# An encoder layer on two requests: projection traced at three times the pace, and two attentions that alternate on score banks of their own

## The chip, the core and the metric

The kernel runs on one NeuronCore of a Trainium2 chip. TensorE (PE; PEld is its weight load) multiplies matrices into PSUM, which has eight banks of 512 float32 values on each of 128 partitions. VectorE (DVE), ScalarE (ACT) and GpSimd (POOL) do the elementwise work, GpSimd only in SBUF. SyncE (SP) and ScalarE issue the DMAs. The engines run side by side, each through its own queue in order, and wait for each other by semaphores. The metric is the device time of one execution in microseconds; shown is the median of the runs.

## The reference

One transformer layer (DEPTH = 1, width 1024) is applied to two requests with the same weights: a prompt of 1024 positions and a sample of 512. Each gets 16 learned meta tokens in front, which are dropped at the end.

```python
n = rms_norm(x, g_mix);  proj = n @ w_in            # 18 column tiles of 128
# group A: 8 query heads of 64 on 2 key heads, per-head RMS norm of q and k, 2-D rotary
s = einsum('bqhgd,bkhd->bhgqk', qblk, ka) * scale;  oa = softmax(s) @ va
# group B: 4 heads, two softmax maps each, 1-D rotary
a = softmax(s0) - lam * softmax(s1);  ob = rms_norm(a @ vb, g_subln) * (1 - lam_init)
x = x + concat(oa, ob) @ w_out
n = rms_norm(x, g_ffn)
gate = conv3(n @ w_ff_gate) + conv_b                # width 3 over positions
x = x + (gelu(gate) * (n @ w_ff_up)) @ w_ff_down    # d_ff = 2816
return rms_norm(x, g_final)[:, N_META:]
```

## The kernel before

All is float32. A dense matmul takes each operand as a rounded part and a remainder (`split`, lines 120 to 124; hi on ScalarE, lo on VectorE or GpSimd) and sums three products (`mm3`, lines 127 to 131: hi·hi, hi·lo, lo·hi). Its lines 129, 130 and 131 stand for all dense work, and the tile name tells which: `ps_mm<-xhi,w_hi`, `ps_p`, `ps_mm<-a_hi,w_hi` (the last product of the feed-forward).

In the code s = 0 is the prompt and s = 1 the sample. The parts are generators, and each `yield` gives the columns that TensorE went through:

- `projection(s)`, lines 157 to 371: RMS statistics, then the 18 column tiles of `w_in`, with rotary and head norm on the other engines. q, k and v go to DRAM as hi and lo parts (SP, lines 258 and 345 to 353).
- `attention(s)`, lines 374 to 588. `softmax` (line 419) is given 128 queries (or 102 to 114 in group B): scores against all keys into one wide PSUM tile (lines 426 and 427; two banks for the sample, three for the prompt), the eviction with scale and row maximum on VectorE (line 430), the exponential on ScalarE (line 433). `weighted_v` (line 436) transposes the probabilities through `ps_t` (line 447), splits them (lines 123 and 124) and multiplies with v into one `ps_o` bank (lines 457 to 462, the tail at 471). Group A goes in blocks of 512 queries (lines 509 to 544): 8 for the sample, 16 for the prompt, and two short blocks each for one halo position. Group B (lines 546 to 588) adds two scalings on ScalarE (lines 553 and 556) and a sum on GpSimd (line 557) for each tile, and a norm of the output (lines 562 to 569), whose sum of squares takes the `ps_o` bank once more (line 566): 8 blocks for the sample, 12 for the prompt. q, k and v are loaded from DRAM on SP (lines 395, 414 and 416).
- `mixer_out(s)`, lines 609 to 668: the output projection and the residual, with h loaded from DRAM (line 640).
- `conv_glu(s)`, lines 671 to 798: the feed-forward in groups of two d_ff tiles, and the final norm.

`trunk_kernel` strings them together (lines 914 to 949). The sample's projection runs first. Then `merge` (line 801) traces the sample's attention beside the prompt's projection, 1 to 1.1 by columns, the projection 20,000 columns ahead; it ends with the attention, and the rest of the projection is drained. Then `merge` traces the prompt's attention beside the sample's `mixer_out` and `conv_glu`, 1 to 1, the attention 60,000 columns ahead; the rest of those is drained. The prompt's `mixer_out` and `conv_glu` come last and alone.

The traced order isn't the order of the instructions. It is a priority: a planner (`schedule_with_timeline_sim`) goes through a simulated time and gives each engine the first instruction in this order that is ready. `issue_after` forbids to issue before a given instruction on the same engine.

PSUM comes in pools that are opened and closed in the order of tracing. While both run, the sample's attention and the prompt's projection hold 2 banks for scores, 2 for `ps_t`, 1 for `ps_o` and 3 for `ps_mm`. After that, the prompt's attention has 3 for scores, 2 and 1, and the dense work beside it has 2. All these pools are closed and opened anew between the two stages, in one stack.

Of the kernel before, what the change touches and what calls it, by code (L numbers as in the profile page):

```python
# [12 lines left out]
F32 = mybir.dt.float32  # L13
# [4 lines left out]
PSUM = bass.MemoryType.PSUM  # L18
DRAM = bass.MemoryType.DRAM

P = 128
# [52 lines left out]
class Psum:  # L74


    def __init__(self, tc, name, **bufs):
        self.tc, self.name, self.count = tc, name, 0
        self.es, self.last = ExitStack(), ExitStack()
        self.pools = {tag: self.open(self.es, tag, b) for tag, b in bufs.items()}  # L80

    def open(self, es, tag, bufs):
        self.count += 1
        return es.enter_context(self.tc.tile_pool(name=f"{self.name}{self.count}_{tag}", bufs=bufs, space=PSUM,
                                                  reuse_waits="tile"))

    def relay(self, **bufs):
        self.last.close()
        for tag, b in bufs.items():
            self.pools[tag] = self.open(self.last, tag, b)  # L90

    def close(self):
        self.last.close()
        self.es.close()

    def tile(self, rows, cols, tag):
        return self.pools[tag].tile([P, 512], F32, name=f"ps_{tag}", tag=tag)[:rows, :cols]

    def wide(self, rows, chunks, cols):

        return self.pools["s"].tile([P, chunks, 512], F32, name="ps_s", tag="s")[:rows, :, :cols]


def pool(ctx, g, name, bufs, side):
# [269 lines left out]
def attention(ctx, g, s, side):  # L374
    nc, tc = g.nc, g.tc
# [3 lines left out]
    nch = -(-n // 512)  # L379
# [39 lines left out]
    def softmax(q, k, l):  # L419

        M = q[0].shape[-1]
        p = pp.tile([P, ne], F32, name="p", tag="p")[:M]
        ps = g.psum.wide(M, nch, kw)
        for i in range(nch):
            kc = k[:, i * kw:(i + 1) * kw]
            nc.tensor.matmul(ps[:, i], lhsT=q[0], rhs=kc, start=True, stop=False)  # L426
            nc.tensor.matmul(ps[:, i], lhsT=q[1], rhs=kc, start=False, stop=True)  # L427

        nm = sp.tile([P, 1], F32, name="nm", tag="nm")[:M]
        g.evicted = nc.vector.tensor_scalar(out=p.rearrange("p (i w) -> p i w", i=nch), in0=ps, scalar1=-HD ** -0.5,  # L430
                                            scalar2=3.0e38, op0=ALU.mult, op1=ALU.min, accum_out=nm).ins
        p = p[:, :n]
        nc.scalar.activation(p, p, AF.Exp, bias=nm, scale=-1.0, accum_out=l)  # L433
        return p

    def weighted_v(pl, v, diff):

        W = sum(p.shape[0] for p in pl)
        o = g.psum.tile(P, W, "o")
        v, v_tail = v  # L440

# [356 lines left out]
        yield 4 * cw  # L798


def merge(g, a, wa, b, wb, lead, hold):

    done = [0.0, lead]
    after, held = None, 0
    while True:
        i = 0 if b is None or done[0] / wa <= done[1] / wb else 1
        if i == (lead > 0) and held < hold:
            after, held = after or g.mark, held + 1
            order = g.tc.issue_after(after)
        else:  # L810
            order = nullcontext()
        try:
            with order:
                done[i] += next((a, b)[i])
        except StopIteration:
            if i == 0:
                break
            b = None


def drain(gen):
    for _ in gen:
        pass
# [3 lines left out]
PADD = 8  # L827
ML = 2
NRAW, NW = 2, 3
R1, R2 = (1.0, 1.1), (1.0, 1.0)  # L830
LEAD1, LEAD2, HOLD, STATS = -20000.0, 60000.0, 4, 26


@with_exitstack
def trunk_kernel(ctx, tc, g):
# [75 lines left out]
        st.tail = hp  # L911
        return st

    g.psum = Psum(tc, "psa", mm=3)
    g.psum.relay(p=3, t=2)
    with ExitStack() as es0:
        p0 = projection(es0, g, 0, "left", "mm", "mm")
        with ExitStack() as es:
            p1 = projection(es, g, 1, "right", "p", "t")
            for _ in range(STATS):  # L920
                next(p1)
            next(p0)
            drain(p1)
        g.psum.relay(s=1, t=2, o=1)
        with ExitStack() as es1:
            merge(g, attention(es1, g, 1, "right"), R1[0], p0, R1[1], LEAD1, HOLD)
        drain(p0)
    g.psum.close()
    g.psum = Psum(tc, "psb", mm=2)
    g.psum.relay(s=1, t=2, o=1)  # L930
    with ExitStack() as es1:
        st1 = state(es1, 1, "right", True)

        def sample():
            yield from mixer_out(g, 1, st1, "right", True, "mm")
            yield from conv_glu(es1, g, 1, st1, "right", 1)
        f1 = sample()
        with ExitStack() as es0:
            merge(g, attention(es0, g, 0, "left"), R2[0], f1, R2[1], LEAD2, HOLD)
        drain(f1)  # L940
        g.psum.relay(s=6)
        st0 = state(ctx, 0, "left", False)
        drain(mixer_out(g, 0, st0, "left", False, "s"))
    xp = pool(ctx, g, "fx0", 1, "right")
    st0.x = [xp.tile([P, KT, SEQS[0] + 2], F32R, name=nm) for nm in ("xhi", "xlo")]
    g.psum.close()
    g.psum = Psum(tc, "psc", mm=8)
    drain(conv_glu(ctx, g, 0, st0, "right", 2))
    g.psum.close()


def rope_tables():
# [60 lines left out]
```

## Time and profile before

| | |
|---|---|
| Median of 3 runs | 2235.35 us (2234.18 to 2236.82) |
| Profiled execution | 2229.83 us; its span, first to last instruction, 2228.0 us |
| Mean granted TensorE clock | 0.977 |
| Instructions | 32312, of them 12442 matmuls |
| HBM read, written | 172.11 MB, 48.55 MB |

The profiled execution is one of its own, and all times in the views are counted from its first instruction. "Busy" of TensorE is modelled from start and size of each matmul, and a matmul at a lower granted clock is busy for longer; so busy time times granted clock is what was done at full speed. In a windows view, a row gives for a stretch its width, the busy time of each engine with the number of instructions in brackets, the granted clock (1.00 is full), the share of DMA engines busy, and GB/s. In a timeline, a row gives start, length, engine, line, operation and count, and in brackets how long the engine had been idle and what released it.

### The profile page before, as it was taken

Reading aid. Unit: us, or ns where it says so; the run is one execution under the profiler, and the core shown is the slowest. Engines: PE = TensorE matmul, PEld = TensorE weight load, DVE = VectorE, ACT = ScalarE, POOL = GpSimd, SP = SyncE. Lnnn points to the kernel's source line nnn. Section 1 sums busy time; section 2 is a strip of 40 time slices with the busy share of each in tenths; the row PEclk is TensorE's granted clock in tenths of the full one; section 3 lists DMA queues with packets and bytes.
Section 4 is the critical chain, followed back from the end, with each engine's and each line's share of the span. In section 5 each row is a group of like instructions: output and inputs, shape, how many; then the busy total and the mean of one; then the engine's idle time right before and its main releaser. Section 6 shows DMA issues by size and latency. Waiting matters only on the chain.

```text
span 2228.0 us, 32312 instructions
## 1 busy us (share of the span) xinstructions
PE 2131.8 (96%) x12442; PEld 1912.6 (86%) x12442; DVE 1269.7 (57%) x2235; ACT 1039.7 (47%) x1830; POOL 668.5 (30%) x514
## 2 busy tenths in 40 slices
PE   7898999986999999999999998999999999999997
PEld 6897999975898888889989986998888888888887
DVE  6535554454767677777777775774443344433346
ACT  6434555565656445567777775552112221112224
POOL 5862446431123111144444433330111000111004
PEclk9999999996999999999999998999999999999999
DMA  6663454443332322223333215621111111111112
GB/s 216 195 206 116 143 169 162 134 162 116 124 99 73 101 79 81 85 72 117 111 101 99 77 61 180 197 94 47 43 37 54 48 48 48 48 38 57 48 39 76
DMA packets 109794, 222.77 MB, mean 100 GB/s; under 512 B 11976, under 2 KB 63048, under 8 KB 109128
## 3 DMA queue, kind: packets, MB, share of 16 engines
q1 hardware_dynamic: 80840, 115.83, 15.9%
q10 hardware_dynamic: 28800, 104.87, 14.9%
q8 instruction: 98, 1.61, 0.3%
q14 instruction: 56, 0.46, 0.1%
HBM read 172.11 MB, written 48.55 MB: 99 GB/s over the span
## 4 chain that ended last, share of the span: by engine, by line
PE 83%; DVE 6%; DMA 3%; ACT 3%; issue 3%; POOL 1%; SPq 1%; ACTq 0%; DVEq 0%; POOLq 0%
PE ps_mm L129 20%; PE ps_mm L130 20%; PE ps_mm L131 20%; PE ps_t L447 5%; PE ps_s L426 4%; PE ps_s L427 3%; PE ps_o L462 2%; PE ps_o L461 2%; DVE p L430 1%; PE ps_p L129 1%; PE ps_p L131 1%; PE ps_p L130 1%; DMA q<-qk 1%; PE ps_o L457 1%; PE ps_o L459 1%
## 5 line engine op out<-in xcount | busy, mean ns | idle before, releaser
L129 PE MATMUL ps_mm<-xhi,w_hi 128*128 128x512 f32 (+6 forms) x1968 | 664.1, 338 | 3.1 <-DVE hn L115 2.5
L130 PE MATMUL ps_mm<-xlo,w_hi 128*128 128x512 f32 (+6 forms) x1968 | 658.1, 335 | 0.0
L131 PE MATMUL ps_mm<-xhi,w_lo 128*128 128x512 f32 (+6 forms) x1968 | 657.2, 334 | 0.0
L129 PEld LDWEIGHTS ps_mm<-xhi,w_hi 128*128 128x128 f32 x1968 | 372.8, 190 | 30.1 <-DVE hn L115 3.1
L131 PEld LDWEIGHTS ps_mm<-xhi,w_lo 128*128 128x128 f32 x1968 | 372.7, 189 | 24.8 <-issue 0.2
L130 PEld LDWEIGHTS ps_mm<-xlo,w_hi 128*128 128x128 f32 x1968 | 372.9, 190 | 24.2 <-POOL xlo L124 0.2
L123 ACT CAST w_hi<-w_f 128x1024 fp32r<-128x1024 f32 x134 | 139.3, 1048 | 393.5 <-PE ps_mm L130 357.9
L430 DVE TENSOR_SCALAR_CACHE_REDUCE p<-ps_s 114x1044 f32<-114x1044 f32 (+5 forms) x212 | 223.4, 1054 | 137.8 <-PE ps_s L427 111.2
L124 POOL TENSOR_TENSOR a_lo<-gate,a_hi 128x512 fp32r<-128x512 f32 x66 | 98.9, 1499 | 649.3 <-ACT a_hi L123 648.3
L123 ACT CAST pt_hi<-ps_t 128x512 fp32r<-128x512 f32 (+6 forms) x360 | 169.7, 483 | 202.1 <-PE ps_t L447 180.7
L433 ACT ACTIVATE p<-p,nm 114x1040 f32<-114x1040 f32 (+5 forms) x212 | 215.2, 1015 | 82.0 <-DVE p L430 78.8
L749 DVE TENSOR_TENSOR h<-ps_mm,h 128x512 f32<-128x512 f32 (+1 forms) x288 | 182.3, 645 | 122.9 <-PE ps_mm L131 122.2
L124 DVE TENSOR_TENSOR pt_lo<-ps_t,pt_hi 128x512 fp32r<-128x512 f32 (+4 forms) x312 | 172.0, 564 | 130.9 <-ACT pt_hi L123 129.2
L130 PE MATMUL ps_mm<-a_lo,w_hi 128*128 128x512 f32 (+1 forms) x576 | 216.0, 378 | 0.0
L131 PE MATMUL ps_mm<-a_hi,w_lo 128*128 128x512 f32 (+1 forms) x576 | 215.5, 377 | 0.0
L129 PE MATMUL ps_mm<-a_hi,w_hi 128*128 128x512 f32 (+1 forms) x576 | 214.9, 385 | 0.4 <-DVE h L749 0.4
L426 PE MATMUL ps_s<-k,q 128*114 128x348 f32 (+4 forms) x552 | 181.2, 333 | 31.8 <-DMA q<-qk 19.0
L447 PE MATMUL ps_t<-ident,p 128*128 128x128 f32 (+7 forms) x1188 | 183.3, 270 | 3.2 <-ACT r_rows L482 2.9
L427 PE MATMUL ps_s<-k,q 128*114 128x348 f32 (+4 forms) x552 | 175.0, 322 | 4.9 <-DMA q<-qk 4.9
L447 PEld LDWEIGHTS ps_t<-ident,p 128*128 128x128 f32 (+7 forms) x1188 | 142.5, 136 | 32.1 <-issue 5.0
L124 DVE TENSOR_TENSOR w_lo<-w_f,w_hi 128x1024 fp32r<-128x1024 f32 x100 | 123.3, 1242 | 81.6 <-ACT w_hi L123 81.2
L557 POOL TENSOR_TENSOR p<-p 114x1040 f32<-114x1040 f32 (+2 forms) x56 | 114.9, 2051 | 124.4 <-ACT p L556 122.5
(194 smaller groups left out, 3539.3 us busy)
## 6 DMA issues: line engine op xcount, KB each, us to landing
w_f<-w_gate ACTq DMA_DIRECT2D x44, 512.0 KB
w_f<-w_up ACTq DMA_DIRECT2D x44, 512.0 KB
w_f<-w_down ACTq DMA_DIRECT2D x44, 512.0 KB
w_f<-w_in ACTq DMA_DIRECT2D x36, 512.0 KB
w_f<-w_out ACTq DMA_DIRECT2D x32, 512.0 KB
q<-qk SPq DMA_DIRECT2D x48, 257.0 KB
q<-qk SPq DMA_DIRECT2D x48, 171.0 KB
qk<-hi SPq DMA_DIRECT2D x20, 384.0 KB
```

The lines of the kernel that those rows point to most:

```text
L123: return (nc.scalar.copy(hi, src), (lo_engine or nc.vector).tensor_tensor(out=lo, in0=src, in1=hi.bitcast(F32), op=ALU.subtract))
L124: (lo_engine or nc.vector).tensor_tensor(out=lo, in0=src, in1=hi.bitcast(F32), op=ALU.subtract))
L129: nc.tensor.matmul(ps, lhsT=whi, rhs=xhi, start=start, stop=False)
L130: nc.tensor.matmul(ps, lhsT=whi, rhs=xlo, start=False, stop=False)
L131: return nc.tensor.matmul(ps, lhsT=wlo, rhs=xhi, start=False, stop=stop).ins
L426: nc.tensor.matmul(ps[:, i], lhsT=q[0], rhs=kc, start=True, stop=False)
L427: nc.tensor.matmul(ps[:, i], lhsT=q[1], rhs=kc, start=False, stop=True)
L430: g.evicted = nc.vector.tensor_scalar(out=p.rearrange("p (i w) -> p i w", i=nch), in0=ps, scalar1=-HD ** -0.5, scalar2=3.0e38, op0=ALU.mul ...
L433: nc.scalar.activation(p, p, AF.Exp, bias=nm, scale=-1.0, accum_out=l)
L447: nc.tensor.transpose(tps[:, c:c + M], p[:, k0:k0 + kw], g.ident[:M, :M])
L557: nc.gpsimd.tensor_tensor(out=p0, in0=p0, in1=p1, op=ALU.add)
L749: nc.vector.tensor_tensor(out=hs, in0=ps, in1=hs, op=ALU.add)
```

## The change

Nothing is computed in another way; what changes is the order of tracing, and which PSUM banks belong to whom.

- `merge` for the sample's attention and the prompt's projection goes at 1 to 3 (before 1 to 1.1), and ends when the projection ends (`until=1`), not the attention.
- The three `ps_mm` banks of the projection are then closed, and in their place a pool `s0` of three banks for the prompt's scores is opened. The sample's own two banks `s1`, the two `ps_t` banks and the one `ps_o` bank stay open.
- A new `merge` traces the rest of the sample's attention beside the prompt's attention, 1 to 1, the sample 12,000 columns ahead, until the sample's ends. `ps_t` and `ps_o` are shared by both; `g.busy` is set from the opening of a `ps_o` tile to the next `softmax`, and with `whole=True` the tracing doesn't change streams in between.
- `s1` is closed then, and two `ps_mm` banks are opened for the sample's dense work. The last `merge`, of the prompt's attention and that work, has a lead of 30,000 (before 60,000).
- `Psum` keeps one stack per tag and a side for each pool, so that a single pool can be closed.

```diff
     def softmax(q, k, l):
...
-        ps = g.psum.wide(M, nch, kw)
+        ps = g.psum.wide(M, nch, kw, f"s{s}")
+        g.busy = False
...
     def weighted_v(pl, v, diff):
...
+        g.busy = True
         o = g.psum.tile(P, W, "o")
...
-def merge(g, a, wa, b, wb, lead, hold):
+def merge(g, a, wa, b, wb, lead, hold, whole=False, until=0):
     done = [0.0, lead]
-    after, held = None, 0
+    after, held, i = None, 0, 0
     while True:
-        i = 0 if b is None or done[0] / wa <= done[1] / wb else 1
+        if not (whole and g.busy):
+            i = 0 if b is None or done[0] / wa <= done[1] / wb else 1
...
         except StopIteration:
-            if i == 0:
+            g.busy = False
+            if i == until:
                 break
+            assert i == 1
             b = None
...
-R1, R2 = (1.0, 1.1), (1.0, 1.0)
-LEAD1, LEAD2, HOLD, STATS = -20000.0, 60000.0, 4, 26
+R1, R2, R3 = (1.0, 3.0), (1.0, 1.0), (1.0, 1.0)
+LEAD1, LEAD2, LEAD3, HOLD, STATS = -20000.0, 12000.0, 30000.0, 4, 26
...
-        g.psum.relay(s=1, t=2, o=1)
-        with ExitStack() as es1:
-            merge(g, attention(es1, g, 1, "right"), R1[0], p0, R1[1], LEAD1, HOLD)
-        drain(p0)
-    g.psum.close()
-    g.psum = Psum(tc, "psb", mm=2)
-    g.psum.relay(s=1, t=2, o=1)
...
+    ps.open("t", 2, "right")
+    ps.open("o", 1, "right")
+    ps.open("s1", 1, "right")
+    a1 = attention(es1, g, 1, "right")
+    merge(g, a1, R1[0], p0, R1[1], LEAD1, HOLD, until=1)
+    es0.close()
+    ps.close("mm")
+    ps.open("s0", 1, "left")
+    es0 = ExitStack()
+    a0 = attention(es0, g, 0, "left")
+    merge(g, a1, R2[0], a0, R2[1], LEAD2, HOLD, whole=True)
+    es1.close()
+    ps.close("s1")
+    ps.open("mm", 2, "right")
...
-        with ExitStack() as es0:
-            merge(g, attention(es0, g, 0, "left"), R2[0], f1, R2[1], LEAD2, HOLD)
+        merge(g, a0, R3[0], f1, R3[1], LEAD3, HOLD)
+        es0.close()
         drain(f1)
-        g.psum.relay(s=6)
+        ps.close("s0", "mm", "o", "t")
+        ps.open("s", 6, "left")
```

More of the change, by code (lines that the diff above doesn't have):

```diff
@@ L912, in state @@
         return st
[L914 to L930 removed]
+    ps = g.psum = Psum(tc)
+    g.busy = False
+    es0, es1 = ExitStack(), ExitStack()
+    ps.open("mm", 3, "left")
+    ps.open("p", 3, "right")
+    ps.open("t", 2, "right")
+    p0 = projection(es0, g, 0, "left", "mm", "mm")
+    with ExitStack() as es:
+        p1 = projection(es, g, 1, "right", "p", "t")
+        for _ in range(STATS):
+            next(p1)
+        next(p0)
+        drain(p1)
+    ps.close("t", "p")
+    ps.open("t", 2, "right")
+    ps.open("o", 1, "right")
[11 more added lines that the diff above has]
+    ps.open("mm", 2, "right")
     with ExitStack() as es1:
```

36 lines of the change are left out of this document (15 added, 21 removed).

## The prediction

> **What bounds the kernel now.** I read the page's shares first: TensorE is busy nearly always, so a gain can only come from stretches in which it is not, or runs at a lower clock.
>
> ```profile
> PE 2131.8 (96%) x12442; PEld 1912.6 (86%) x12442; DVE 1269.7 (57%) x2235; ACT 1039.7 (47%) x1830; POOL 668.5 (30%) x514
> ```
>
> Then the windows view, cut at the stages: width, busy time of PE, PEld, DVE, ACT, POOL, clock, DMA.
>
> ```profile
> 151.80:200.00 48.20, 38.49 (x206) 35.35 (x205) 21.73 (x46) 17.60 (x38) 16.29 (x14) 0.86 0.49 154
> 200.00:489.80 289.80, 282.33 (x1834) 266.25 (x1833) 153.26 (x366) 157.02 (x340) 132.62 (x92) 0.99 0.45 146
> 489.80:534.90 45.10, 23.31 (x92) 18.47 (x90) 17.67 (x44) 21.90 (x53) 11.23 (x12) 0.59 0.45 154
> 534.90:585.00 50.10, 44.92 (x244) 36.27 (x245) 37.48 (x75) 37.79 (x80) 2.80 (x3) 0.93 0.37 127
> 1300.00:1350.00 50.00, 42.82 (x273) 36.76 (x271) 30.02 (x58) 30.49 (x59) 11.22 (x8) 0.98 0.28 98
> 1350.00:1400.00 50.00, 44.16 (x217) 40.05 (x218) 29.84 (x49) 27.03 (x57) 22.57 (x21) 0.82 0.52 169
> ```
>
> My measure is **lost time**: width less busy time times clock. It is 15.1 us at 151.8 to 200, 10.3 to 489.8, 45.1 - 23.31 x 0.59 = 31.3 to 534.9, 8.3 to 585, and 8.0 + 13.8 = 21.8 around 1350. So two hand-overs carry the loss: from the projection to the prompt's attention, and from that to the last stage.
>
> The first hand-over, in the timeline (start, length, engine, line, operation, then idle time before it and its releaser):
>
> ```profile
> 489.11 0.29 PE L131 MATMUL ps_mm<-xhi,w_lo 128*128 128x272 f32 x1
> ...
> 510.26 0.52 PE L426 MATMUL ps_s<-k,q 128*102 128x264 f32 x1 [7.20 <-DMA q<-qk]
> ...
> 521.19 0.54 PE L426 MATMUL ps_s<-k,q 128*102 128x264 f32 x1 [4.18 <-DMA q<-qk]
> ...
> 534.88 0.66 PE L426 MATMUL ps_s<-k,q 128*128 128x348 f32 x1 [0.47 <-DVE p L430]
> ```
>
> ```profile
> 490.12 1.95 SPq L395 DMA_DIRECT2D k<-ka  x2
> ...
> 496.41 4.92 SPq L395 DMA_DIRECT2D q<-qk  x3
> 504.42 0.74 SPq L258 DMA_DIRECT2D qk<-hi  x1
> ```
>
> Both programs share L426; the widths tell them apart, 264 for the sample and 348 for the prompt. The projection's last dense matmul is at 489.1. The traced order had put much of the projection behind the sample's attention, but the planner used its ready matmuls as filling, so it ended first. The sample's attention then runs alone for 45 us with holes for q. The prompt's k, v and q were issued from 490 to 501; its first scores come only at 534.9, behind the sample's last eviction (L430): the score banks are the same.
>
> **The change part by part.**
>
> *Pace 1:3.* Yields in the code: a sample head costs 4 x 1056 + 22 x 512 = 15.5 thousand columns in group A and 10 x 1056 + 22 x 514 = 21.9 in group B, 211.6 in all; the projection yields 455.5. From -20 and at a third of the pace, its end stands at (455.5 - 20)/3 = 145 of the sample. 66 thousand columns stay, three B heads or six blocks; before it was about half of that. Nothing is added: matmuls, DMAs and casts are the same in number. The 10.3 us lost beside the projection should shrink a little as less attention lies there: I take **8** (5 to 15; the first 48 us stay at 15.1). POOL's and SP's share of the projection (132.6 us busy of 289.8 on POOL) is compressed by some 10% and stays hidden.
>
> *Score banks of their own (s0 on the mm banks).* The wait for the sample's last eviction goes. What is late next is the load: the k, v and q of the prompt can only be issued when the projection's SBUF is free, at its end, and SP is one queue: 11 us of issues above, then the projection's last store at 504.4. The rows of this hand-over, and of the stretch in which the prompt then runs alone:
>
> ```profile
> 489.80:508.00 18.20, 8.11 (x32) 6.15 (x30) 8.68 (x21) 10.96 (x25) 8.07 (x8) 0.63 0.61 209
> 508.00:534.90 26.90, 15.20 (x60) 12.32 (x60) 8.99 (x23) 10.94 (x28) 3.16 (x4) 0.56 0.34 117
> 551.50:583.50 32.00, 29.61 (x167) 22.92 (x167) 25.49 (x50) 24.24 (x50) 1.29 (x1) 1.00 0.43 141
> ```
>
> The first 18 us (13.1 lost) happen again, since the sample's q loads stand in the same queue: **12** (6 to 18). The 18.4 us lost in 508 to 534.9 go. Prompt alone, until the sample's output projection begins, loses 2.4: **3** (2 to 6).
>
> *The mixed stretch, which is new.* Six B blocks of the sample alternate with the prompt's A blocks; by the lead of 12 the prompt gets 54 thousand columns, 1.8 blocks of 29.8. There is no dense work beside it. Rows for one of each, TensorE first, then ScalarE:
>
> ```profile
> 577.79 0.60 PE L447 MATMUL ps_t<-ident,p 128*128 128x128 f32 x4
> ...
> 578.73 0.60 PE L447 MATMUL ps_t<-ident,p 128*128 128x128 f32 x4
> ...
> 582.15 0.32 PE L427 MATMUL ps_s<-k,q 128*128 128x348 f32 x1
> 582.31 0.32 PE L426 MATMUL ps_s<-k,q 128*128 128x348 f32 x1
> ...
> 1334.09 0.43 PE L471 MATMUL ps_o<-pt_hi,v_tail 96*128 96x342 f32 x1 [0.28 <-ACT pt_hi L469]
> ...
> 1338.92 0.43 PE L457 MATMUL ps_o<-pt_hi,v 128*128 128x342 f32 x1 [1.70 <-DVE o_rs L115]
> ```
>
> ```profile
> 503.17 0.71 ACT L123 CAST pt_hi<-ps_t 128x306 fp32r<-128x306 f32 x2
> 503.77 0.74 ACT L553 ACTIVATE p<-p,r_b 104x528 f32<-104x528 f32 x1
> 504.41 0.73 ACT L556 ACTIVATE p<-p,c 104x528 f32<-104x528 f32 x1
> ...
> 570.08 1.17 ACT L433 ACTIVATE p<-p,nm 128x1040 f32<-128x1040 f32 x1
> 571.15 0.19 ACT L433 ACTIVATION_READ_ACCUMULATOR p<-p,nm 128x1 f32 x1
> 571.24 0.57 ACT L123 CAST pt_hi<-ps_t 128x512 fp32r<-128x512 f32 x1
> ```
>
> TensorE per B head of the sample: 40 score matmuls of 264 columns, 0.12 us apart by the 0.16 of the 348-wide ones (582.15 to 582.31), 4.8; 25 transposes of about 0.1, 2.5; 24 value matmuls of about 0.12, 2.9; the rest 1: 11.2 us, three heads 34. Per A block of the prompt: 24 scores of 0.16 (3.8), eight steps of 0.94 (577.79 to 578.73), the rest 0.6: 12 us, 1.8 of them 22. Sum **56 us**. ScalarE per B head: five tiles, each with two exponentials and two scalings of 0.64 to 0.73, 13.7; eight casts of 0.33, 2.6; tails and norm, some 13 of 0.37, 4.9: 21 us, three heads 63. Per A block: four of 1.16, eight casts of 0.5, the rest 1.3: 9.9, times 1.8 is 18. Sum **81 us**. So ScalarE, not TensorE, sets this stretch: 81 - 56 = 25 lost. Matmuls of the projection covered these exponentials before; that cover is what the new pace gives up. As the planner will slip a little more of the sample beside the projection, I take **24**; the near end is 11 (sample as far as before, ScalarE 33 + 18 against 40 on TensorE), the far end 54: a B block's chain through the one ps_o bank leaves 4.8 us between its last value matmul and the next block's first (1334.09 to 1338.92), and if nothing fills these holes, six add 29 to the 81. It takes the place of 8.3 - 2.4 = 5.9 lost now. The waits for ps_o and ps_t stand in TensorE's one queue: scores of both samples behind them wait too, and the evictions behind those.
>
> *The later lead of 30 instead of 60.* The prompt starts its common run with the sample's dense work further on: 54 thousand columns, and 73 in the 32 us alone (29.61 us busy at 12 a block), 127; now these 73 and a few scores before them. So about 49 thousand fewer are to be paired. The prompt's 800 thousand now last until about 1331, 746 us after 585, near 1 us a thousand, of which 0.4 to 0.5 is its own matmuls and the rest the sample's: when its attention ends, 25 to 30 us of the sample's dense matmuls should be left. Now there is none:
>
> ```profile
> 1300.00:1331.00 31.00, 19.09 (x113) 16.22 (x113) 6.70 (x16) 0.00 (x0) 1.00 0.17 56
> 1331.00:1349.50 18.50, 0.00 (x0) 0.00 (x0) 0.38 (x1) 0.00 (x0) 0.96 0.45 160
> ```
>
> (the same view for ps_mm alone). The 21.8 us lost around 1350 should fall to **8** (4 to 22), the casts of the last stage being what is late next.
>
> **Sum.** Lost now: 10.3 + 13.1 + 18.4 + 5.9 + 2.4 + 21.8 = 71.9. Then: 8 + 12 + 0 + 24 + 3 + 8 = 55. Gain 17 us. The profiled execution took 2229.83 us (span 2228.0, 1.8 around it), so 2213; the median of the runs is 5.5 higher, so **2218**.
>
> **The rivals.**
> - *The pace doesn't take hold.* The planner goes by what is ready, as it did before; the sample is then as far as now when the projection ends. Against it: traced order is still its priority. Mixed loss 14 instead of 24: 2208.
> - *The hole before the last stage stays*, because the prompt's last chain and the loads behind it are late anyway: +14, 2232.
> - *Slower: one chain.* In the mixed stretch both attentions pass ScalarE and one ps_o bank, and neither fills the other's 4.8 us holes: 54 lost instead of 24, 2248. It decides against the change from 41 lost, that is, when the stretch is longer than 97 us. For it: ScalarE's 81 us leave no slack. Against: in 551.5 to 583.5 the prompt alone keeps TensorE at 93%.
> - *The clock.* If the mixed stretch, with many short holes, is granted 0.59 as at 489.8 to 534.9, its 56 us of matmuls take 95, above ScalarE's 81: 39 lost, 2233. Against it: 551.5 to 583.5 has short holes too and was granted 1.00; the 0.59 came with holes of 7.2 and 4.2 us. The Trainium skill, "TensorE: Matmul & The Clock Gate", section "A second HAM failure mode: psum-queue depth-cycling", speaks for this rival: frequent micro-idling between groups of matmuls makes the clock swing between half and full. By that rule the time is 2233 or more; the trace so far disagrees for holes below 1 us.
> - *Better:* the sample's loads pass the hand-over without holes and the mixed stretch is near its lower end: 2196.
>
> **How the numbers follow.** Forecast 0.45 (own range 2205 to 2230), pace without effect 0.15, hole stays 0.12, one chain 0.16, clock 0.05, better 0.07. A measurement of this kernel can tell 0.2%, 4.5 us, from no change. Faster: 0.45 + 0.15 + 0.07, rounded up for part of the second, 0.68; same 0.15; slower 0.17. The range leaves out the ends of the better and the slower case: 2195 to 2245.
>
> **What would show it.** The projection's last dense matmul near 455 to 470 instead of 489; the first 348-wide scores some 20 us later, before the sample's last 264-wide ones; between them a stretch of 70 to 90 us with ScalarE over 85% busy and TensorE near 70%; the sample's first output matmul near 570 to 590; dense matmuls of the sample beside the prompt's last block, and 5 to 10 us lost around it. Wrong if the sample has less than four blocks left at the projection's end, if ScalarE is idle for a third of the mixed stretch, or if TensorE stands at the second hand-over as before.

## The result, and the profile after

The changed kernel takes 2297.67 us (2297.25 to 2299.53, 4 runs) beside 2235.82 for the kernel before: ratio 1.0279 (1.0261 to 1.0297), 62 us slower. The forecast was 2218. The profiled execution took 2297.68 us, 67.9 more than that of before. One execution of a later run, e1, took 4220.5 us and is left out of its median; as it was the profiled one, no view of e1 is used.

From the page of the changed kernel (busy time and share, then the granted clock in 40 slices of 57.4 us):

```profile
span 2295.9 us, 32285 instructions
PE 2144.8 (93%) x12442; PEld 1921.9 (84%) x12442; DVE 1278.8 (56%) x2235; ACT 1039.2 (45%) x1830; POOL 667.7 (29%) x514
PEclk9999999958899999999999997999999999999999
```

The matmuls are the same 12442. The clock dips in the ninth to the eleventh slice (459 to 631 us, the first hand-over and what follows it) and in the 25th, the second hand-over. The windows view cuts the span there, and the lines are renumbered: L421 and L422 are the scores (426 and 427 before), L425 their eviction, L389 the loads of q and k, L601 the mean square of the sample's norms.

```profile
200.00:460.00 260.00, 259.00 (x1663) 244.72 (x1662) 126.18 (x289) 115.36 (x240) 119.15 (x72) 1.00 0.45 146
460.00:532.00 72.00, 28.42 (x107) 22.40 (x106) 17.17 (x49) 25.97 (x60) 11.89 (x14) 0.55 0.40 134
532.00:608.00 76.00, 56.75 (x320) 46.02 (x318) 50.38 (x123) 62.17 (x138) 15.71 (x21) 0.90 0.20 67
608.00:645.00 37.00, 32.59 (x168) 24.13 (x168) 24.52 (x47) 24.99 (x54) 2.55 (x2) 0.92 0.29 88
645.00:760.00 115.00, 110.45 (x775) 101.08 (x776) 82.03 (x156) 70.52 (x140) 32.73 (x37) 0.97 0.30 91
760.00:1300.00 540.00, 535.64 (x3221) 474.20 (x3219) 388.77 (x645) 338.16 (x560) 175.60 (x141) 0.99 0.29 91
1300.00:1385.00 85.00, 84.36 (x527) 76.60 (x526) 61.60 (x101) 56.42 (x92) 33.43 (x25) 1.00 0.23 78
1385.00:1435.00 50.00, 23.12 (x152) 20.71 (x150) 27.25 (x56) 24.90 (x59) 15.01 (x16) 0.71 0.43 147
```

Lost time, by the prediction's measure (width less busy times clock): 1.0 beside the projection, 72 - 28.42 x 0.55 = **56.4** in the hand-over, 24.9 in the mixed stretch (to the value products of the sample's last block but one), 7.0 from there to the sample's first output matmul, about 18 in the common stretch of the prompt's attention and the sample's dense work (7.9, 9.7 and 0.6), and 50 - 23.12 x 0.71 = **33.6** before the last stage. The common stretch of the kernel before lost 3.4:

```profile
583.00:1300.00 717.00, 713.61 (x4461) 636.88 (x4461) 513.24 (x890) 456.09 (x776) 235.50 (x197) 1.00 0.29 91
```

The stretch up to 460 is what the change promised. What it gains there is lost many times over behind it.

The hand-over in the timeline of TensorE (start, length, engine, line, operation; in brackets the idle time before and what ended it):

```profile
463.05 0.34 PE L421 MATMUL ps_s<-k,q 128*104 128x264 f32 x1 [2.46 <-DMA q<-qk]
...
483.06 0.52 PE L421 MATMUL ps_s<-k,q 128*102 128x264 f32 x1 [3.75 <-DMA q<-qk]
...
497.36 0.52 PE L421 MATMUL ps_s<-k,q 128*102 128x264 f32 x1 [9.24 <-DMA q<-qk]
...
527.87 0.52 PE L421 MATMUL ps_s<-k,q 128*104 128x264 f32 x1 [15.50 <-DMA q<-qk]
```

All four are scores of the sample (264 wide) that wait for their queries. The queue that issues those, SyncE's:

```profile
481.89 13.87 SPq L389 DMA_DIRECT2D q<-qk  x6
...
495.81 4.67 SPq L389 DMA_DIRECT2D k<-ka  x2
500.52 4.93 SPq L408 DMA_DIRECT2D v<-v  x2
...
507.90 10.11 SPq L389 DMA_DIRECT2D k<-qk  x3
518.13 5.00 SPq L389 DMA_DIRECT2D q<-qk  x2
```

The first rows are loads of the prompt: queries of three blocks, keys and values of the second key head, and keys of its second attention, which are not needed before 979. They can start once the projection's SBUF is free, which now happens with seven blocks of the sample still to come. The sample's queries come last. An issue of these takes 2.3 us and more (13.87 for six), where six loads of q in a row take 3.63 in e9 below; so the queue is held up by what the DMA engines carry away. Their view for 482 to 535 (busy share in tenths and GB/s in 40 slices, then SyncE's queue):

```profile
DMA  2222222222222229727832222222222222234223
GB/s 92 96 99 98 99 101 104 100 99 96 94 96 104 99 101 211 243 106 216 270 122 100 95 106 98 93 104 104 98 98 104 110 94 87 95 130 155 90 92 111
q1 hardware_dynamic: 3482, 6.08, 33.0%
```

It looks as if the engines had room: two tenths busy. But the rate stands flat near 100 GB/s while loads of q and k are in the queue; the bumps above 200 GB/s follow the two loads of v, issued at 500.5 to 505.5 on the same queue. That is the picture of a transfer that only some four of the 16 engines carry, and in the trace's own packets of this queue four are under way at a time from 482 to 501 (the median). The experiments test it.

The second hand-over, TensorE again:

```profile
1421.86 1.22 PE L601 MATMUL ps_mm<-acc,ones_d 128*128 128x256 f32 x2 [17.85 <-POOL acc L596]
...
1434.01 1.22 PE L601 MATMUL ps_mm<-acc,ones_d 128*128 128x256 f32 x2 [7.48 <-POOL acc L596]
1434.67 0.85 PE L123 MATMUL ps_s<-xhi,w_hi 128*128 128x344 f32 x1
```

The first dense matmul of the last stage (`ps_s<-xhi`) stands right behind the sample's last norm, which waits for squares summed on GpSimd. In the kernel before, the same dense matmuls were issued ahead of that norm and covered it:

```profile
1349.90 0.66 PE L129 MATMUL ps_s<-xhi,w_hi 128*128 128x344 f32 x1 [1.52 <-ACT xhi L123]
...
1369.12 0.59 PE L605 MATMUL ps_mm<-acc,ones_d 128*128 128x256 f32 x2
```

### The profile page after: what moved, and what is told of

It reads as the page before. It is cut to its first block, busy times and chain, and to the rows that moved or that the text cites. A ratio compares the mean times of both kernels' runs of the same rounds, so it can differ in the third digit from the quotient of the medians.

```text
span 2295.9 us, 32285 instructions
## 1 busy us (share of the span) xinstructions
PE 2144.8 (93%) x12442; PEld 1921.9 (84%) x12442; DVE 1278.8 (56%) x2235; ACT 1039.2 (45%) x1830; POOL 667.7 (29%) x514
## 4 chain that ended last, share of the span: by engine, by line
PE 66%; DVE 4%; ACT 2%; issue 1%; DMA 1%; POOL 0%; DVEq 0%; ACTq 0%
PE ps_mm L123 16%; PE ps_mm L124 16%; PE ps_mm L125 16%; PE ps_t L443 4%; PE ps_s L421 2%; PE ps_s L422 2%; PE ps_o L458 1%; PE ps_s L125 1%; PE ps_o L457 1%; PE ps_s L124 1%; PE ps_s L123 1%; DVE p L425 1%; DVE y L771 1%; DVE w_lo L145 1%; PE ps_o L455 1%
## 5 line engine op out<-in xcount | busy, mean ns | idle before, releaser
L123 PEld LDWEIGHTS ps_mm<-xhi,w_hi 128*128 128x128 f32 x1968 | 372.9, 190 | 28.4 <-DVE hn L109 3.1
L124 PEld LDWEIGHTS ps_mm<-xlo,w_hi 128*128 128x128 f32 x1968 | 373.0, 190 | 24.9 <-issue 0.5
L425 DVE TENSOR_SCALAR_CACHE_REDUCE p<-ps_s 114x1044 f32<-114x1044 f32 (+5 forms) x212 | 222.9, 1053 | 122.6 <-PE ps_s L422 91.0
L117 ACT CAST pt_hi<-ps_t 128x512 fp32r<-128x512 f32 (+7 forms) x360 | 169.4, 484 | 173.5 <-PE ps_t L443 154.8
L421 PE MATMUL ps_s<-k,q 128*114 128x348 f32 (+4 forms) x552 | 184.5, 339 | 57.9 <-DMA q<-qk 34.0
L443 PE MATMUL ps_t<-ident,p 128*128 128x128 f32 (+6 forms) x1188 | 187.2, 274 | 9.9 <-DVE pt_lo L118 4.7
L422 PE MATMUL ps_s<-k,q 128*114 128x348 f32 (+4 forms) x552 | 175.8, 324 | 5.6 <-DMA q<-qk 5.6
L443 PEld LDWEIGHTS ps_t<-ident,p 128*128 128x128 f32 (+6 forms) x1188 | 144.3, 138 | 39.4 <-DVE pt_lo L118 6.5
L421 PEld LDWEIGHTS ps_s<-k,q 128*128 128x128 f32 (+3 forms) x552 | 104.0, 188 | 75.1 <-issue 37.6
```

The costliest lines, as they stand in the source:

```text
L117: return (nc.scalar.copy(hi, src), (lo_engine or nc.vector).tensor_tensor(out=lo, in0=src, in1=hi.bitcast(F32), op=ALU.subtract))
L123: nc.tensor.matmul(ps, lhsT=whi, rhs=xhi, start=start, stop=False)
L124: nc.tensor.matmul(ps, lhsT=whi, rhs=xlo, start=False, stop=False)
L443: nc.tensor.transpose(tps[:, c:c + M], p[:, k0:k0 + kw], g.ident[:M, :M])
```

## Experiments

| run | kernel | us | ratio to before (95%) |
|---|---|---|---|
| e1 | before, pace 3.0 | 2284.6 | 1.0226 (1.0209 to 1.0243) |
| e2 | changed, pace 2.2 | 2269.1 | 1.0162 (1.0146 to 1.0177) |
| e3 | changed, some sample loads from ScalarE | 2300.0 | 1.0296 (1.0281 to 1.0312) |
| e4 | changed, prompt's loads held back | 2308.9 | 1.0335 (1.0318 to 1.0352) |
| e5 | before, pace 0.6 | 2235.1 | 1.0003 (0.9991 to 1.0014) |
| e6 | changed, last stage on own banks | 2282.2 | 1.0208 (1.0190 to 1.0226) |
| e7 | changed, prompt's loads from GpSimd | 2300.1 | 1.0292 (1.0275 to 1.0309) |
| e8 | changed, prompt's loads in turn | 2290.9 | 1.0246 (1.0226 to 1.0266) |
| e9 | changed, new order in DRAM | 2245.0 | 1.0052 (1.0037 to 1.0067) |
| e10 | **before, new order in DRAM** | **2201.4** | **0.9853 (0.9835 to 0.9870)** |
| e11 | e9 and e6 | 2233.3 | 0.9999 (0.9989 to 1.0008) |
| e12 | e11, pace 2.2 | 2218.6 | 0.9926 (0.9906 to 0.9946) |
| e13 | e11, lead 60 | 2219.6 | 0.9938 (0.9921 to 0.9954) |
| e14 | e10, lead 30 | 2213.6 | 0.9904 (0.9887 to 0.9921) |
| e15 | changed, no scalings | 2281.9 | 1.0215 (1.0192 to 1.0237) |
| e16 | e10, lead 90 | 2207.1 | 0.9878 (0.9859 to 0.9897) |
| e17 | e11, pace 2.2, lead 60 | 2204.7 | 0.9871 (0.9857 to 0.9886) |
| e18 | changed, lead 60 | 2277.9 | 1.0197 (1.0180 to 1.0214) |

### Pace: e1, e2, e5

```diff
 # e1, in the kernel before          # e5: (1.0, 0.6)
-R1, R2 = (1.0, 1.1), (1.0, 1.0)
+R1, R2 = (1.0, 3.0), (1.0, 1.0)
 # e2, in the changed kernel
-R1, R2, R3 = (1.0, 3.0), (1.0, 1.0), (1.0, 1.0)
+R1, R2, R3 = (1.0, 2.2), (1.0, 1.0), (1.0, 1.0)
```

> The kernel before with the one number changed, 1 to 3 instead of 1 to 1.1; the prompt's scores still wait for the sample's last eviction. Theory A (what costs is the sample's attention that is left without dense work beside it, and the alternation saves part of that): projection ends near 460, the sample then alone for 90 us or more, 2300 to 2340 us. Theory B (the pace is harmless, the alternation itself costs): 2225 to 2245.

> The changed kernel at 1 to 2.2: by columns 14 thousand of the sample's attention are left at the projection's end instead of 66. Theory A: most of the loss beside both attentions goes, 2235 to 2260 us. Theory B (banks, shared ps_o and order cost by themselves): 2280 or more.

> The kernel before with the opposite pace: the prompt's projection is traced at 0.6 columns for one of the sample's attention, instead of 1.1; nothing else changes. Theory A (each block of the sample that is left when the projection ends costs some 12 us, because nothing dense covers its loads and exponentials): three or four blocks fewer are left than before, the hand-over's 31 us of loss fall to 5 to 15, and the time is 2205 to 2220. Theory B (the kernel before has its pace where the sum of both sides is least: the covered stretch itself gets longer when more exponentials stand in it): 2235 to 2260.

Each of the first two fell between its theories. The pace alone costs 51 us in the old structure, where nothing can alternate. At 2.2 the projection ends at 481.7 with four blocks of the sample left, as before, and the changed kernel still loses 36. So the pace does a good part of the damage, 29 us of it in the changed kernel, but not all. e5 says nothing on the theories: four blocks are left there too (their last value matmuls at 495, 520, 541 and 558), so the planner went by what was ready, and the slower pace did not take hold.

### The loads of the hand-over: e3, e4, e7, e8

```diff
 # e3: another queue for the sample's loads
-        nc.sync.dma_start(out=tl.bitcast(F32), in_=parts[:, m, :, c0:c0 + cw])
+        q = nc.scalar if s == 1 and j >= KB else nc.sync
+        q.dma_start(out=tl.bitcast(F32), in_=parts[:, m, :, c0:c0 + cw])
 # e4: the prompt's loads held behind a store of its own (g.stored, SyncE)
+        with tc.issue_after(g.stored) if s == 0 and kv else nullcontext():
             k = load_k(KA, kv)
             v = load_v(0, P, kv * P)
...
+        with tc.issue_after(g.stored) if s == 0 and h == 0 else nullcontext():
             ks = [load_k(KB + h // 2 * 2, h % 2 * 2 + m) for m in range(2)]
             v = load_v(1 + h, 2 * P, 0)
 # e7: another queue for the prompt's first loads (k, v, three q)
+        early = nc.gpsimd if s == 0 else nc.sync
...
 # e8: as e4, but behind the loads of the block before (loaded), and the
 #     third block's q behind the first block's sums (told)
+        with tc.issue_after(loaded) if s == 0 and kv else nullcontext():
...
+                with tc.issue_after(told) if s == 0 and kv == 0 and i * nblk + b == 2 else nullcontext():
                     q = load_q(QA + 2 * kv, i, NMETA + 512 * b - 2, 514)
```

> The changed kernel, with the sample's group B q and k loads issued from ScalarE's queue, so that they don't stand behind the prompt's prefetch in SP's queue. If the order in SP's queue makes the holes after the projection's end: of 60 us lost between 460 and 532 some 25 to 35 come back, 2265 to 2275 us. If the DMA engines' rate makes them: within 10 us of the changed kernel, 2288 to 2300.

> The changed kernel, with the prompt's loads that are not needed yet held back: k and v of its second key head until the first head's last store but one, k and v of its first B head until group A's. About 3 MB fewer go through SP's queue ahead of the sample's q. If prefetch is what the sample waits for, by order or by rate: 20 to 35 us come back, 2262 to 2278 us. If the sample waits for its own chain: within 5 us of 2298.

> The changed kernel, with the prompt's first loads (its first three pairs of queries, both key heads' keys and values, and the first keys of its second attention) issued from GpSimd's queue; the sample's loads stay on SyncE's. Theory A (the hand-over's holes are an order of the queue: the sample's queries stand behind the prompt's loads on SyncE): the holes of 9 and 15 us go, the sample's first output matmul is at 620 to 632 instead of 645, and the time is 2270 to 2285. Theory B (the transfers themselves are slow there, as all of them share the DMA engines, whatever the queue): the holes stay, 2293 to 2303. Theory C (the queue of GpSimd now holds up the sample's own steps there): above 2305.

> The changed kernel, with the prompt's early loads put in turn on SyncE's queue: the third block's queries behind the first block's store of sums, the second key head's keys and values behind the queries of the block before it, the first keys of the second attention likewise. Theory A (order of the queue): the 15 us hole goes and the 9 us one shrinks by a third, and unlike the coarser hold nothing is given back at the prompt's later heads: 2275 to 2285. Theory B (what is won at the hand-over is lost later whatever the hold, since the common stretch is bound by something else): 2293 to 2310.

e3 does not test what its expectation says: QB is 6 and KB is 10, so the edit moved the sample's keys alone, and its queries stayed on SyncE; of the queries it shows nothing. e4 and e8 take the hole of 15.5 us away, and the one of 9.2 stays (9.3 and 9.6); the row of e4 for the hand-over:

```profile
460.00:532.00 72.00, 40.38 (x190) 33.64 (x190) 30.91 (x81) 39.33 (x91) 14.46 (x18) 0.64 0.39 128
```

TensorE is busy 40.4 us there, not 28.4. In e4 the sample's first output matmul comes 16 us earlier (629.3 beside 644.9), but the held loads are then late for the prompt's second key head and its second attention (TensorE waits 1.6 and 4.6 us for them, and not at all in the changed kernel), and the end is 11 us later, which neither of its answers had. e8 holds them less long and keeps 7 us, between its theories. So the order of SyncE's queue is part of it and not the whole: in e7 the prompt's loads are out of that queue, and as much is lost, though in other holes. The longest, of 16.6 us, still ends on a load of queries, and SyncE takes 7.3 us to issue two of them; one of 8.8 us is new and waits for a sum on GpSimd, whose queue now has the loads too, so that e7 isn't a clean test of the queue. Its DMA view, 462 to 545:

```profile
q0 software_dynamic: 4224, 4.85, 28.8%
q1 hardware_dynamic: 3562, 4.38, 17.7%
...
q<-qk POOLq DMA_DIRECT2D x6, 257.0 KB, 18.6
```

The queries that GpSimd issued (its queue is q0) needed 18.6 us to land. Another queue issues the work; the same DMA engines carry it. The Trainium skill says so on its page "DMA: Bandwidth & Descriptors", section "Issuing engines are not separate DMA queues", and this run is in line with it: the time did not fall.

### The rate of a load: e9, e10, e11

In DRAM, the 128 rows that a head's load takes were four groups of 32, far apart. e9 lays them one behind the other, so that a load is one plain run of 128 rows; the store of a plane is cut in four for it.

```diff
-        parts = src[first:first + 2].rearrange("p x (m r) n -> (p x) m r n", r=32)
-        nc.sync.dma_start(out=tl.bitcast(F32), in_=parts[:, m, :, c0:c0 + cw])
+        parts = src[m, first:first + 2].rearrange("p x r n -> (p x r) n")
+        nc.sync.dma_start(out=tl.bitcast(F32), in_=parts[:, c0:c0 + cw])
...
-            nc.sync.dma_start(out=to, in_=part.bitcast(F32))
+            for a in range(4):
+                if y.shape[1] == 2:
+                    to = dst[a, i, :, :, c0:c0 + cw].rearrange("x r n -> r x n")
+                else:
+                    to = dst[a % 2, i, a // 2, :, c0:c0 + cw][:, None]
+                nc.sync.dma_start(out=to, in_=part[a * 32:(a + 1) * 32].bitcast(F32))
...
-        g.qk.append([dram.tile([3, 2, P, n], F32, name=f"qk{s}_{i}") for i in range(len(PAIRS))])
-        g.ka.append(dram.tile([2, 2, HD, n], F32, name=f"ka{s}"))
+        g.qk.append([dram.tile([4, 3, 2, 32, n], F32, name=f"qk{s}_{i}") for i in range(len(PAIRS))])
+        g.ka.append(dram.tile([2, 2, 2, 32, n], F32, name=f"ka{s}"))
```

> The changed kernel with another order of the queries and keys in DRAM: the 128 rows that one load takes for a head now lie one behind the other, where they were four groups of 32; the store of each plane is cut in four DMAs of 32 rows for that. Nothing else changes. In the runs so far only four packets of such a load are under way at a time, and SyncE's queue moves 95 to 105 GB/s in the hand-over, as stores go up to 280. Theory A (the hand-over is bound by this rate: the prompt's first loads and the sample's queries, some 4 MB, pass at 100 GB/s): the rate between the projection's end and 530 is above 200 GB/s, the holes of 9 and 15 us go, the hand-over's loss falls from 56 to 25 to 35, and the time is 2260 to 2280 beside 2298. Theory B (it is the chain of short blocks itself, whatever the loads): 2292 to 2305. Theory C (the stores, four times as many, delay the projection): above 2305.

> The kernel before with the same order in DRAM, and nothing else. It loses 31 us in its hand-over, 21 of them in waits for queries. Theory A (rate of the loads): 2210 to 2225, faster than before. Theory B: 2230 to 2240. Theory C: above 2240.

> The changed kernel with both edits: the order in DRAM, and the last stage's own three banks. If the hole at the hand-over and the one at 1400 have different causes, the gains add: the gain of the first alone plus 15.5 us, so 2245 to 2265. If they feed one another, the sum is less by 5 us or more. Either way, what is left above the kernel before (10 to 30 us) is the price of the mixed stretch and of the common one.

This is the largest single cause: 52.7 us in the changed kernel, 33 in the kernel before, both beyond what theory A gave. Of the 53 us, 34 are in the hand-over, where e9 loses 37 - 22.98 x 0.63 = 22.5 (447 to 484), and 7 in the first 48 us of the sample's attention, which has the same loads (14.6 lost from 151.8 to 200, 7.4 in e9); the rest lies in small pieces. The DMA view of e9, 447 to 500:

```profile
DMA  9998995006659998999999999964975000759800
GB/s 181 258 377 234 244 321 201 20 29 161 152 113 190 392 292 322 373 398 394 352 368 372 386 291 385 390 256 96 260 183 201 14 0 5 232 99 341 273 0 0
q1 hardware_dynamic: 7873, 11.04, 64.8%
```

The same loads now go at some 290 to 400 GB/s with the engines nine tenths busy, where they went at 100 with two tenths, and sixteen packets of the queue are under way at a time (464 to 481, the median), where it was four. The prompt's first scores come at 484 and no longer at 530, and the sample's first output matmul at 597.4 and no longer at 644.9. The Trainium skill has the rule on the page "DMA: Bandwidth & Descriptors", section "Rules for kernel authors": the outermost dimension of a transfer's access patterns bounds the engines that carry it, so one of size 4 confines it to four. The two views agree with it. It stands on a page that the prediction did not bring to bear on its rows.

e10 beats both kernels of this study: 1.5% faster than before. e11's two gains nearly add (52.7 and 15.5 alone, 64.4 together); its time lies below the forecast range only because e9 gained more than forecast.

### The banks of the last stage: e6

```diff
-        ps.close("s0", "mm", "o", "t")
-        ps.open("s", 6, "left")
+        ps.close("s0")
+        ps.open("s", 3, "left")
...
-    ps.close("s")
+    ps.close("s", "mm", "o", "t")
```

> The changed kernel, in which the prompt's output projection gets the three banks that the prompt's own attention leaves, instead of six that overlap those of the sample's dense work; the sample's banks stay allotted until it ends. Theory A (the hole around 1400 comes from the new order of the banks: the six banks of the last stage reach over those in which the sample's norm still waits for GpSimd): the first dense matmul of that stage is issued before the sample's last two norm matmuls, the stretch's 33.6 us of loss fall to 10 to 20, and the time is 2275 to 2288 beside the change's 2298. Theory B (the hole comes from the casts and loads of the last stage, which are late anyway): 2293 to 2303, with the first dense matmul still behind the hole.

Theory A, with its numbers: 15.5 us. From the timeline of e6:

```profile
1406.84 0.42 PE L123 MATMUL ps_s<-xhi,w_hi 128*128 128x344 f32 x1 [1.52 <-ACT xhi L117]
...
1425.55 0.59 PE L601 MATMUL ps_mm<-acc,ones_d 128*128 128x256 f32 x2
```

The last stage begins 18.7 us before the sample's last norm and covers it. In the change, its six banks began at the bottom of PSUM and reached over the two in which that norm was still to be written; the dense matmuls of the last stage had to stand behind it. Of the 33.6 us lost from 1385 to 1435, e6 loses 50 - 41.48 x 0.86 = 14.3.

### What is left: e12 to e18

e12, e13 and e17 change the numbers of e11, e14 and e16 the lead of e10, e18 the lead of the changed kernel:

```diff
-R1, R2, R3 = (1.0, 3.0), (1.0, 1.0), (1.0, 1.0)
+R1, R2, R3 = (1.0, 2.2), (1.0, 1.0), (1.0, 1.0)
 # e12, e17
-LEAD1, LEAD2, LEAD3, HOLD, STATS = -20000.0, 12000.0, 30000.0, 4, 26
+LEAD1, LEAD2, LEAD3, HOLD, STATS = -20000.0, 12000.0, 60000.0, 4, 26
 # e13, e17, e18
 # e14, e16: LEAD2 (60000 before) is 30000, 90000
```

> The changed kernel with the new order in DRAM and the last stage's own banks, at a pace of 2.2 instead of 3.0: four blocks of the sample are left at the projection's end, as in the kernel before, so that hardly more than the alternation remains of the change. The kernel before with the same order in DRAM took 2201. Theory A (the pace, by the blocks that it leaves uncovered and ScalarE's work in them, is the rest of the loss): 2205 to 2215. Theory B (the alternation itself costs, since both attentions pass one ps_o bank and ScalarE): 2220 to 2235, no better than at the pace of 3.0, 2233.

> The changed kernel with the new order in DRAM and the last stage's own banks, and the sample's lead over the prompt in the common stretch back at 60 thousand columns, as in the kernel before. Theory A (the lead of 30 costs in the common stretch, where 9 us more are lost than before, and gives at its end): the common stretch wins 5 to 9, its end loses up to 5: 2225 to 2233 beside 2233. Theory B (the lead has no effect, the order is the planner's): 2231 to 2236.

> The kernel before with the new order in DRAM, and the lead of its second merge 30 thousand instead of 60. If dense matmuls of the sample are then left beside the prompt's last block, the 25 us lost around the end of the prompt's attention shrink by 8 to 15: 2186 to 2195 beside 2201. If the prompt's attention merely starts later by as much, 2198 to 2206.

> The kernel before with the new order in DRAM, and the lead of its second merge 90 thousand columns instead of 60. A lead of 30 took 2213.6 and one of 60 2201.4: from 30 to 60 the last blocks of the prompt's attention were better covered. If that goes on, 2188 to 2196; if the best lies near 60, as the sample's dense work then runs out before the prompt's attention ends, 2200 to 2215.

> The changed kernel with the new order in DRAM, the last stage's own banks, the pace of 2.2 and the lead of 60 thousand: all that is left of the change is that the prompt's attention may stand between the sample's heads, in banks of its own. If pace and lead are the whole of the 32 us that were open, it comes to the 2201 of the kernel before with the same loads: 2198 to 2208. If the alternation has a price of its own, 2211 to 2220.

> The changed kernel with the lead of the common stretch back at 60 thousand columns, and nothing else. With the new order in DRAM and the last stage's own banks the same edit was worth 13.7 us. If the lead is a cause of its own, 2280 to 2288 beside 2298. If it only helps where the last stage has its own banks, 2293 to 2300.

The lead of 30 is a loss wherever it was tried: 12.2 us (e14 less e10), 13.7 (e11 less e13), 13.9 (e12 less e17), 19.7 (changed less e18). Whether 60 is better than 90 is not shown: e16 is 5.7 us behind e10 in the median, but their runs overlap (2200.3 to 2210.1 and 2196.0 to 2204.6). Of the expectations, e17 came as its first answer said and e16 as its second, e12 fell between its theories, e13 and e18 gained more than forecast, and e14 lost 12 us where neither of its answers had more than 5. Part of the loss shows in the common stretch, first e11 with a lead of 30, then e13 with 60:

```profile
597.00:1310.00 713.00, 703.66 (x4368) 627.86 (x4368) 517.56 (x876) 451.42 (x770) 234.75 (x197) 0.99 0.29 90
```

```profile
609.00:1290.00 681.00, 677.45 (x4241) 608.39 (x4240) 495.57 (x851) 450.16 (x761) 239.87 (x196) 0.99 0.29 91
```

TensorE stands idle for 9.3 us in the first and 3.6 in the second. The changed kernel and e18 show the same, 9.3 (645 to 1360) and 3.6 (662 to 1330). The rest of the 14 lies in the two neighbouring stretches. Before the common one, from 446 on, e11 loses 151 - 118.31 x 0.80 = 56.4 and e13 163 - 127.46 x 0.86 = 53.4; behind it, up to 1400, 90 - 80.32 x 0.92 = 16.1 and 110 - 101.64 x 0.97 = 11.4. Why the order of a lead of 30 covers less stays open.

The pace of 3.0 instead of 2.2 costs 14.7 us (e11 less e12) and 14.9 (e13 less e17) once the loads are wide, but 28.6 with the loads as they were (changed less e2). With both back, e17 is at 2204.7, and e10, which has no alternation, at 2201.4; their intervals overlap. So at a pace of 2.2 the alternation on banks of its own costs next to nothing, and it gains nothing. At 3.0 it may gain: e18 differs from e1 by the alternation and by the last stage's banks, which cost by themselves, and is 6.7 us faster, with intervals that just touch.

The runs thus give a path from the kernel before to the changed one: wide loads -33.1 (from the 2234.5 of the kernel before beside e10), alternation +3.3, lead +13.9, pace +14.7, the last stage's banks +11.7, narrow loads +52.7. Together they are the whole difference, +63.2 with this kernel before and 61.9 with the one of the result; that they add up follows from how the path is built, and each size holds for its place in it. So the narrow loads cost 20 us more in the changed kernel than before, and the pace of 3.0 twice as much beside narrow loads as beside wide ones.

### ScalarE in the mixed stretch: e15

The sample's second attention here leaves out its two scalings by the sums, so its probabilities are subtracted unscaled.

```diff
-            nc.scalar.activation(p0, p0, AF.Copy, scale=r[:, 0:1])
+            if s == 0:
+                nc.scalar.activation(p0, p0, AF.Copy, scale=r[:, 0:1])
...
-            nc.scalar.activation(p1, p1, AF.Copy, scale=c)
+            if s == 0:
+                nc.scalar.activation(p1, p1, AF.Copy, scale=c)
```

> The changed kernel without the two scalings on ScalarE in the sample's second attention (the two maps' probabilities are subtracted unscaled): 1.4 us of ScalarE per tile less, everything else is kept. Theory A (two limits one after the other: the loads up to 532, ScalarE from there to the sample's end at 608): the waits for queries before 532 stay within 5 us of 34, and from the first 348-wide scores to the sample's last block it takes 60 to 66 us instead of 76; in all 2278 to 2292. Theory B (the mixed stretch is bound by the chain through the one ps_o bank and not by ScalarE): that part stays within 4 us of 76, 2292 to 2300.

```profile
535.00:608.00 73.00, 55.12 (x310) 45.23 (x308) 47.29 (x118) 48.51 (x116) 16.33 (x21) 0.90 0.21 70
```

The time is in theory A's range, but the mechanism is not. In e15 the prompt's first scores (511.6) come ahead of the last long hole (16.9 us, ended at 532.2), so the stretch is counted from behind that hole, as in the changed kernel. ScalarE's work in it falls from 62.2 to 48.5 us and the stretch only from 76 to 73 (by 6 us, counted from the very end of the hole); lost time is 23.4 instead of 24.9. So ScalarE alone does not set it. Nor does this run show that the one `ps_o` bank does: in the changed kernel TensorE's longest sum of waits from 535 to 645 is 10.4 us, for evictions of scores (L425), each attention having one score tile. What the stretch is bound by stays open. Most of what e15 gained came behind the stretch, in the common one (643 to 1392, in the changed kernel 645 to 1404, for the prompt's attention to end): 10 of the 14 us between the two profiled executions. Its cause is not shown.

## Why the prediction was wrong

- *Pace.* Right in what it does: the last dense matmul at 459.0 (455 to 470 forecast), seven blocks left (six), 1.0 us lost beside the projection (8).
- *Hand-over.* **The step that failed first**: "The first 18 us (13.1 lost) happen again, since the sample's q loads stand in the same queue: **12** (6 to 18). The 18.4 us lost in 508 to 534.9 go." In place of these 12 it measured 56.4, and the prompt's first scores came 71 us after the projection's end, not 20. The step put the second part down to the shared score banks and so at nothing. TensorE's waits in the kernel before, from 489.8 to 534.9, are others (in us: the sum, how often, the longest):

```profile
PE ps_s L426 <- DMA q<-qk: 15.0, 3, 7.2
PE ps_s L427 <- DMA q<-qk: 2.8, 3, 1.1
PE ps_s L426 <- DVE p L430: 2.0, 4, 0.8
```

  Queries cost 17.8 us there and evictions of scores 2.0; the holes of 7.20 and 4.18 us in the prediction's own rows end on `DMA q<-qk`. New banks don't touch that loss, and the change put more into the stretch: seven blocks of the sample with their queries in place of four, and all of the prompt's early loads. The row that should have warned was quoted: 508 to 534.9 had a DMA share of 0.34 and 117 GB/s. e9 and e10 show that this rate was the limit.
- *Mixed stretch.* 24 forecast, 24.9 measured, and that is luck. The sum counted six blocks of the sample; four had their value products in this stretch, two had them in the hand-over and one behind it. The reason is not shown either: ScalarE was 82% busy, and taking 22% of its work away changed the stretch by 3 to 6 us.
- *Prompt alone.* 3 forecast, 7.0 measured: small. The prompt is not alone there, as the sample's last block has its value products at 625 to 631.
- *The common stretch.* The sum has no term for it. It lost 3.4 us before and about 18 now, which is the third largest part of the difference; with the lead back at 60 (e18), TensorE's idle time in it falls from 9.3 to 3.6.
- *The later lead and the last stage.* The second failure: "The 21.8 us lost around 1350 should fall to **8**". It measured 33.6. The mechanism was there, dense matmuls of the sample did lie beside the prompt's last blocks (TensorE busy 84.4 of 85 us from 1300 to 1385), but the hole moved behind them, for the order of the banks, which the prediction did not price; without it e6 loses 14.3, inside the step's range of 4 to 22. And the lead itself, counted as a gain of 14, is a loss of 12 to 20 in all four pairs.
- *The rivals.* "One chain" gave the right sign at the wrong place. "The hole before the last stage stays" came true, for another reason than the one given. The clock's 0.55 fell in the hand-over with its long holes; the mixed stretch, with some twenty holes below 1.6 us and one of 3.6, was granted 0.90: 0.50 at 563.1 to 566.5, at 587.0 to 593.8 and from 604 on, and the full clock in nearly all the rest. So the swing between half and full that the prediction weighed (the Trainium skill, "TensorE: Matmul & The Clock Gate", section "A second HAM failure mode: psum-queue depth-cycling") is there for some 14 of the 76 us, and not at the price of 0.59 that the rival gave it.

## What to carry to other kernels

Before work is moved into a stretch, read what ends its holes; here the rows named loads, and the prediction priced banks. Where it waits for loads, read their rate, not the DMA share: here a share flat at two tenths with a flat 100 GB/s was a full pipe of four engines, and the outermost dimension of the load was where to look. What frees a buffer or a bank earlier also starts its loads earlier, ahead of others that are needed sooner. When PSUM banks are dealt anew, compare which instruction the next stage's first write now has to follow, and price each changed number of a schedule alone: here one change held four (pace, lead, banks, alternation), of which three cost 12 to 29 us each and the last, at a pace of 2.2, nothing.

## What was not expected of the hardware

- A load of 128 rows in four groups of 32 moved at about 100 GB/s with DMA engines at two tenths; the same bytes as one run of 128 rows at some 290 to 400 GB/s with nine tenths.
- Cutting each store of q and k in four, four times as many issues on SyncE, cost nothing that shows: in e9 the projection ends at 447.2, and not later than the 459.0 of the changed kernel.
